# Seven block products instead of eight for a decoder layer's convolution operands and gates, with the gates kept in DRAM

## The chip, the cores and the metric

The kernel runs on one core of a Trainium2 chip. The metric is the device time of one execution in microseconds (us). Before the change it is 2046.91 us, the median of three runs (2045.77 to 2047.66).

## What is computed

One decoder layer for a prompt of 1024 tokens and 8 sample tokens, all in float32. The model width is 1024, and the 1032 tokens are the columns of every product below. Cut to what matters here:

```
p = h @ w_in                                # -> q | k | v | c_b | c_c | c_h | g_a | g_c
u = c_c * c_h
c = (c_b * causal_conv3(u)) @ w_conv_o
a = merge_of_three_attention_groups(q, k, v) @ w_attn_o
mix = (sigmoid(g_a) * a + sigmoid(g_c) * c) @ w_o
x = x + rms_norm(mix)
y = x + rms_norm(square(relu(rms_norm(x) @ w_ff1)) @ w_ff2)
```

Outputs are y for both groups, the updated key and value caches (for the samples a large copy from the input caches with one new row), and the last rows of u.

## The kernel before, in words

Every weight tile is 128 outputs of one matrix by 512 inputs (half of the 1024). `fetch` (L121) loads it with SP (256 KB, at most three raw tiles ahead). `split` (L129) makes two parts of it, so that three fast matmuls give float32 accuracy: ACT casts the high part (`wh`, L134), DVE or POOL subtracts to get the low part (`wl`, L135). The activations are held in two parts as well (`hh`, `hl` for the normalised input). `mac` (L162) issues wh by hh (L165), wh by hl (L168), wl by hh (L169), each 128 by 128 by 344 columns, since the 1032 columns are done in three chunks. `project` runs one tile of 128 outputs: 8 blocks of inputs, 3 chunks, 3 matmuls, so 72 matmuls of 344 columns. `plan` is the list of all weight tiles in the order of use; `tick`, called once per unit of PE work, splits the next tile when a buffer is free (five in `wpool`, two more in `wextra`).

The stages stand one after the other:

- Attention, with projections put between its heads as filling work. The last head has four raw gates as filling (`gate_raw`, L447): the pre-activation is stored in `gc_d` in DRAM.
- Convolution: 24 tiles of w_in, three for each of 8 output tiles (c_c, c_h, c_b). ACT copies c_c, DVE multiplies c_h by it into `E`, two scalar_tensor_tensor operations (L920, L921) do the width-3 convolution, DVE multiplies by c_b, and the result is split into `cvh`, `cvl`. `sample_steps` is a generator with the sample tokens' attention; `drive` pulls a step of it at every second unit of PE work. POOL multiplies cache tiles by queries (L788) and by weights (L844), DVE reduces them (L793) and adds them (L853).
- `wco`: the convolution's output matrix, 8 tiles. Its gates come from `gc_d` (four, loaded on POOL's queue, L953) or are computed in place (four).
- `wao`: the attention's output matrix, 8 tiles of 36 matmuls, with 8 gates between them. At its head the attention's numerators and denominators are loaded (SP), multiplied, and split into `ah`, `al` (L994 to L1000).
- `wo` and the feed-forward part, which the change leaves alone.

`copy_piece` (L278) issues pieces of the cache copy, DRAM to DRAM, 1 MB each, on ACT's queue: 16 in the attention, 16 in the convolution, 8 in `wco`, 8 in `wao`, 9 later. Each engine runs its own instructions in the order in which they stand; the DMA queues of SP, ACT and POOL are in order as well.

Of the kernel before, what the change touches and what calls it, by code (L numbers as in the profile page):

```python
# [19 lines left out]
KT = 8  # L20
# [3 lines left out]
CH = T // 3  # L24
EPS = 1e-6
# [10 lines left out]
def tile_decoder_layer(  # L36
# [10 lines left out]
    gc_d = dram.tile([NRAW, P, T], F32, name="gc_d")  # L47
# [35 lines left out]
    warr = {"win": win, "wao": wao, "wco": wco, "wo": wo, "wf1": wf1, "wf2": wf2}  # L83
    plan = []

    def plan_tiles(name, *ms):
        plan.extend((name, m, i) for m in ms for i in range(warr[name].shape[2] // 4))
# [7 lines left out]
    plan_tiles("win", *range(36, 60))  # L95
    for i in range(KT):
        if i >= NRAW:
            plan_tiles("win", 60 + i)
        plan_tiles("wco", i)
    plan_tiles("win", 68)  # L100
    for i in range(KT):
        if i + 1 < KT:
            plan_tiles("win", 69 + i)
        plan_tiles("wao", i)
    plan_tiles("wo", *range(KT))
    plan_tiles("wf1", 0, 1, 2, 3)
    for pr in range(NP - 2):
        if pr:
            plan_tiles("wf1", 2 * pr + 2, 2 * pr + 3)
        plan.extend(("wf2", 2 * pr + a, hf) for hf in range(2) for a in range(2))  # L110
    plan_tiles("wf1", 2 * NP - 2, 2 * NP - 1)
    plan.extend(("wf2", 2 * pr + a, hf) for hf in range(2) for pr in (NP - 2, NP - 1) for a in range(2))
    plan.reverse()

    spaces = [[wpool, 5, 5]]
    raws, ready = [], []
    clock, turn = [0], [0]
    lo_eng = [nc.gpsimd]
    lo_pin = [lambda ins: ins]

    def fetch():  # L121
        if plan and len(raws) < 3:
            key = plan.pop()
            name, m, i = key
            raw = wpool.tile([P, 4, P], F32, name="wr", tag="wr", bufs=3)
            pin(nc.sync.dma_start(raw, warr[name][m][:, 4 * i:4 * i + 4, :]))
            raws.append((key, raw, clock[0]))
# [10 lines left out]
    def split_next():  # L138
        key, raw, _ = raws.pop(0)
        space = max(spaces, key=lambda e: e[2])  # L140
        turn[0] += 1
        ready.append((key, split(raw, space, lo_eng[turn[0] % len(lo_eng)], lo_pin[0])))

    def tick():
        clock[0] += 1
        if raws and clock[0] - raws[0][2] >= 2 and max(e[2] for e in spaces) > 0:
            split_next()
        fetch()

    def take(key):  # L150
        if not ready:
            if not raws:
                fetch()
            split_next()
        k, w = ready.pop(0)
        assert k == key, (k, key)
        return w
# [103 lines left out]
    hpool = h_stack.enter_context(tc.tile_pool(name="hpool", bufs=1))  # L261
# [16 lines left out]
    def copy_piece(n=1):  # L278
        for _ in range(n):
            if pieces:  # L280
                tc.keep_in_program_order(nc.scalar.dma_start(*pieces.pop(0)))


    with ExitStack() as st:
# [161 lines left out]

        def gate_raw(i):  # L447

            t = aw.tile([P, T], F32, name="vT", tag="v01", bufs=1)

            def use(c, ps):
                nc.scalar.copy(t[:, chunk(c)], ps)
            yield from project(("win", 60 + i), h_in, use)
            nc.scalar.dma_start(gc_d[i], t)
# [211 lines left out]
        def fill(h):  # L666
# [10 lines left out]
            else:  # L677
                for i in range(NRAW):
                    yield from gate_raw(i)
# [30 lines left out]

    def sample_steps(sp):
# [10 lines left out]
        for g in range(3):  # L722
            qt, kt = tile512(NB), tile512(NB)
            for i in range(2):
                ps = bank(at, [P, 4, 2, 64], "ps_tq")
# [10 lines left out]
        for i in range(3):  # L736
            ps = bank(at, [P, 4, 2, 64], "ps_tq")
# [63 lines left out]
        ps = bank(at, [P, 512], "ps_sm")  # L801
# [5 lines left out]
        ps = bank(at, [P, 512], "ps_sm")  # L807
# [15 lines left out]
        ps = bank(at, [P, 512], "ps_sm")  # L823
# [5 lines left out]
        po = bank(at, [P, 512], "ps_so")  # L829
# [44 lines left out]
        ps = bank(at, [P, 512], "ps_sm")  # L874
# [5 lines left out]
    W0 = 36  # L880
    cv_stack = ExitStack()
    cpool = cv_stack.enter_context(tc.tile_pool(name="cpool", bufs=1))
    ch_ = cpool.tile([P, KT, T], F32R, name="cvh")
    cl_ = cpool.tile([P, KT, T], F32R, name="cvl")
    spaces.append([ctx.enter_context(tc.tile_pool(name="wextra", bufs=1, side="right")), 2, 2])
    lo_pin[0] = pin
    with ExitStack() as st:
# [7 lines left out]
        E = cw.tile([P, 2 + T], F32, name="E")  # L895
        nc.vector.memset(E[:, 0:2], 0.0)
        steps = sample_steps(cw)
        lo_eng[:] = [nc.vector, nc.gpsimd]

        short = [None]  # L900

        def drive(g):
            for j, _ in enumerate(g):
                if j % 2 == 1 or short[0]:
                    short[0] = next(steps, None)
        for i in range(KT):
            cs_sb = cw.tile([P, T], F32, name="cs_sb", bufs=1)

            def use_c(c, ps):
                nc.scalar.copy(cs_sb[:, chunk(c)], ps)  # L910
            drive(project(("win", W0 + 3 * i), h_in, use_c))
            def use_h(c, ps):
                nc.vector.tensor_tensor(E[:, 2 + c * CH:2 + (c + 1) * CH], ps, cs_sb[:, chunk(c)], op=OP.mult)
            drive(project(("win", W0 + 3 * i + 1), h_in, use_h))
            nc.scalar.copy(up[:, i, :], E[:, NQ:NQ + 2])
            nc.scalar.copy(us[:, i, :], E[:, NQ + 2:])
            y = cw.tile([P, T], F32, name="yc", bufs=1)
            w0, w1, w2 = (cwt[:, j, i:i + 1] for j in range(3))
            nc.scalar.activation(y[:, 0:NQ], E[:, 0:NQ], AF.Copy, scale=w0)
            nc.vector.scalar_tensor_tensor(y[:, 0:NQ], E[:, 1:1 + NQ], w1, y[:, 0:NQ], op0=OP.mult, op1=OP.add)  # L920
            nc.vector.scalar_tensor_tensor(y[:, 0:NQ], E[:, 2:2 + NQ], w2, y[:, 0:NQ], op0=OP.mult, op1=OP.add)  # L921
            nc.vector.tensor_scalar(y[:, NQ:], stt[:, i, 0, :], w0, None, op0=OP.mult)
            nc.vector.scalar_tensor_tensor(y[:, NQ:], stt[:, i, 1, :], w1, y[:, NQ:], op0=OP.mult, op1=OP.add)
            nc.vector.scalar_tensor_tensor(y[:, NQ:], us[:, i, :], w2, y[:, NQ:], op0=OP.mult, op1=OP.add)

            def use_b(c, ps):
                nc.vector.tensor_tensor(y[:, chunk(c)], ps, y[:, chunk(c)], op=OP.mult)
                nc.scalar.copy(ch_[:, i, chunk(c)], y[:, chunk(c)])
                nc.vector.tensor_tensor(cl_[:, i, chunk(c)], y[:, chunk(c)], ch_[:, i, chunk(c)].bitcast(F32),
                                        op=OP.subtract)  # L930
            drive(project(("win", W0 + 3 * i + 2), h_in, use_b))
# [5 lines left out]
    W1 = W0 + 24  # L937
    m2_d = dram.tile([KT, P, T], F32, name="m2_d")

    def gate(pool, src, store):  # L940
        def use(c, ps):
            s = pool.tile([P, CH], F32, name="sg", tag="sg", bufs=4)
            nc.scalar.activation(s, ps, AF.Sigmoid)  # L943
            store[c] = s
        return project(src, h_in, use)

    lo_eng[:] = [nc.vector]
    with tc.tile_pool(name="sgc", bufs=1, side="right") as sgp:
        for i in range(KT):
            sg = {}  # L950
            if i < NRAW:
# [398 lines left out]
```

## Time and profile before

| what | before |
|---|---|
| median of three runs | 2046.91 us |
| the profiled execution, its own time | 2046.12 us |
| its span in the profile | 2043.3 us |
| mean granted clock of the TensorE | 0.987 of full speed |
| PE busy | 1992.4 us, 12845 instructions |
| DVE, ACT, POOL busy | 1065.7, 687.3, 513.9 us |
| DMA | 195.50 MB, mean 96 GB/s |

A profiled time is made of the span and 2.8 us around it. Engines: PE is the matmul, PEld its weight load, DVE the vector engine, ACT the scalar engine, POOL the GpSimd engine, SP the engine that issues most loads. Matmuls are pipelined, so a matmul's own duration overlaps its neighbours', and what one costs is the distance between two starts. A granted clock of 1.00 is 2.4 GHz, one of 0.50 is 1.2 GHz.

### The profile page before, as it was taken

How to read it: one execution, taken by the hardware profiler on the slowest of the kernel's cores; microseconds unless marked ns; L12 is line 12 of the kernel's file. 1: busy time of each engine (PE TensorE's matmuls, PEld its weight loads, DVE VectorE, ACT ScalarE, POOL GpSimd, SP SyncE). 2: the span in 40 equal slices, each digit the busy share in tenths (PEclk: the TensorE clock that was granted, in tenths of full speed). 3: DMA queues.
4: the chain of work that ended last, by engine and by line, in shares of the span. 5: the costliest groups of instructions: out<-in, count | busy, mean ns of one | idle time of the engine just before them, and what ended most of it. 6: DMA issues, size and time to landing. Idle time of an engine off the chain costs nothing. (4 is left out here: it accounts for less than half of the span.)

```text
span 2043.3 us, 31854 instructions
## 1 busy us (share of the span) xinstructions
PE 1992.4 (98%) x12845; PEld 1971.1 (96%) x12845; DVE 1065.7 (52%) x1837; ACT 687.3 (34%) x1359; POOL 513.9 (25%) x414
## 2 busy tenths in 40 slices
PE   7999999999999999999989999899999999999997
PEld 6999999999999999999989999899999999999996
DVE  7688768777753454632223222825544444444445
ACT  4355435544443122222123233543222222222233
POOL 3233314332334433520013222312111111111113
PEclk8999999999999999999999999999999999999998
DMA  4221222123325644445364431322221111111112
GB/s 145 59 66 38 87 68 66 58 87 98 98 76 169 218 150 162 153 146 190 114 177 149 138 127 46 93 83 93 94 83 53 42 52 42 42 52 52 42 32 83
DMA packets 89667, 195.50 MB, mean 96 GB/s; under 512 B 23488, under 2 KB 33856, under 8 KB 88624
## 3 DMA queue, kind: packets, MB, share of 16 engines
q1 hardware_dynamic: 78144, 116.97, 18.2%
q10 hardware_dynamic: 6672, 63.49, 9.4%
q0 software_dynamic: 4704, 13.01, 2.1%
q8 instruction: 100, 1.64, 0.3%
q14 instruction: 47, 0.39, 0.1%
HBM read 173.60 MB, written 74.29 MB: 121 GB/s over the span
## 5 line engine op out<-in xcount | busy, mean ns | idle before, releaser
L165 PE MATMUL ps_mm<-hh,wh 128*128 128x344 f32 x1824 | 593.5, 325 | 4.7 <-ACT sg L943 2.2
L168 PE MATMUL ps_mm<-hl,wh 128*128 128x344 f32 x1824 | 586.5, 322 | 3.7 <-DVE hl L248 1.9
L169 PE MATMUL ps_mm<-hh,wl 128*128 128x344 f32 x1824 | 585.6, 321 | 0.0
L135 POOL TENSOR_TENSOR wl<-wr,wh 128x512 fp32r<-128x512 f32 x177 | 234.8, 1327 | 868.1 <-ACT wh L134 828.6
L134 ACT CAST wh<-wr 128x512 fp32r<-128x512 f32 x320 | 195.3, 619 | 568.9 <-PE ps_mm L168 477.0
L165 PEld LDWEIGHTS ps_mm<-hh,wh 128*128 128x128 f32 x1824 | 346.1, 190 | 7.4 <-ACT hh L254 2.9
L168 PEld LDWEIGHTS ps_mm<-hl,wh 128*128 128x128 f32 x1824 | 345.7, 190 | 6.0 <-DVE hl L248 3.2
L169 PEld LDWEIGHTS ps_mm<-hh,wl 128*128 128x128 f32 x1824 | 345.7, 190 | 0.0
L165 PE MATMUL ps_mm<-gh,wh 128*128 128x344 f32 x768 | 246.2, 321 | 0.0
L169 PE MATMUL ps_mm<-rh,wl 128*128 128x344 f32 x768 | 246.2, 321 | 0.0
L165 PE MATMUL ps_mm<-rh,wh 128*128 128x344 f32 x768 | 246.1, 320 | 0.0
L169 PE MATMUL ps_mm<-gh,wl 128*128 128x344 f32 x768 | 245.4, 319 | 0.0
L168 PE MATMUL ps_mm<-gl,wh 128*128 128x344 f32 x768 | 245.3, 319 | 0.0
L168 PE MATMUL ps_mm<-rl,wh 128*128 128x344 f32 x768 | 245.3, 319 | 0.0
L1187 DVE TENSOR_TENSOR f<-ps_mm,f 128x344 f32<-128x344 f32 x336 | 167.3, 513 | 97.0 <-PE ps_mm L169 96.8
L1125 DVE TENSOR_TENSOR r<-r 128x344 f32<-128x344 f32 x96 | 59.6, 621 | 215.9 <-ACT rh L1124 215.9
L135 DVE TENSOR_TENSOR wl<-wr,wh 128x512 fp32r<-128x512 f32 x143 | 99.9, 703 | 128.3 <-ACT wh L134 128.0
L168 PEld LDWEIGHTS ps_mm<-gl,wh 128*128 128x128 f32 x768 | 144.7, 188 | 0.0
L169 PEld LDWEIGHTS ps_mm<-gh,wl 128*128 128x128 f32 x768 | 144.7, 188 | 0.0
L165 PEld LDWEIGHTS ps_mm<-gh,wh 128*128 128x128 f32 x768 | 144.7, 188 | 0.0
L165 PEld LDWEIGHTS ps_mm<-rh,wh 128*128 128x128 f32 x768 | 144.5, 188 | 0.0
L169 PEld LDWEIGHTS ps_mm<-rh,wl 128*128 128x128 f32 x768 | 144.5, 188 | 0.0
(259 smaller groups left out, 2943.3 us busy)
## 6 DMA issues: line engine op xcount, KB each, us to landing
wr<-in_win_dram SPq DMA_DIRECT2D x152, 256.0 KB, 2.9
wr<-in_wf_dram SPq DMA_DIRECT2D x128, 256.0 KB, 2.8
out_okv_dram<-in_cache_dram ACTq DMA_DIRECT2D x16, 1020.0 KB, 8.1
kt<-in_cache_dram SPq DMA_DIRECT2D x32, 256.0 KB, 3.8
x_sb<-in_xT_dram SPq DMA_DIRECT2D x12, 344.0 KB, 5.4
m_d<-m POOLq DMA_DIRECT2D x8, 516.0 KB, 7.6
m2c<-m_d POOLq DMA_DIRECT2D x24, 172.0 KB, 3.6
xk<-in_xT_dram SPq DMA_DIRECT2D x12, 344.0 KB, 3.6
```

What stands on the lines that cost most here:

```text
L134: pin_(nc.scalar.copy(hi, raw))
L135: pin_(eng.tensor_tensor(lo, raw, hi.bitcast(F32), op=OP.subtract))
L165: ins = nc.tensor.matmul(ps, wh, rh, start=(first and i == 0), stop=False)
L168: nc.tensor.matmul(ps, wh, rl, start=False, stop=False)
L169: nc.tensor.matmul(ps, wl, rh, start=False, stop=(last and i == n - 1))
L1125: pin(nc.vector.tensor_tensor(r, r, r, op=OP.mult))
L1187: pin(nc.vector.tensor_tensor(d, ps, d, op=OP.add))
```

## The change

Two weight tiles (256 outputs) are taken together, with the inputs in two halves of 512 and the columns in two halves of 516 (`HT`), each done as two slices of 258 (`ST`). A product of two-by-two blocks then takes seven block products instead of eight (Strassen's scheme in the form with four sums of blocks on each side). This is done for 17 pairs: 12 of the convolution's operands (per two output tiles: two pairs "u", whose halves are multiplied together, and one pair "y" with the c_b of both), and 5 of gates ("g"). A pair is 7 products, each 2 slices by 4 blocks by 3 matmuls: 168 matmuls of 258 columns.

- The right-hand sums T1 to T4 are made once, from `hh` and `hl`, by `tsums` on DVE and POOL, while PE computes two gates in the old way (`plain`, tiles 68 and 69). T2, T3, T4 get buffers of their own, T1 takes the place of h in half of `hh` and `hl` (L995, L996), since the seven products read h itself only three times.
- The left-hand sums of a pair are four `combine` operations on POOL (L133): s1, s2, and two in place. Each of the seven forms is then split as before, the low part on DVE alone.
- `strassen` keeps three sums A, B, C in PSUM (two slices each, six banks); ACT copies A, DVE adds the others on the way out. All gates and the convolution's product go to DRAM (`g_d`, `cv_d`) in halves, on POOL's queue, and the attention's heads are split (`split_heads`) beside the last two gate pairs.
- Then `wao` runs first (its gates from `g_d` on POOL's queue, the convolution's product from `cv_d` on ACT's queue, split there), its result goes to `m2_d`, and `wco` follows, with gate and `m2_d` chunks loaded on POOL's queue.
- The cache copy's pieces: 16 in the attention, 30 in the pairs' stage, four together after the last pair, seven in `wao`.

```diff
+    def forms_of(key):
+        ...
+        def s2(r):
+            s[1] = combine("s1", r[0], r[2], OP.add)
+            s[2] = combine("s2", s[1], r[1], OP.subtract)
+            return s[2]
+        how = (((0, 1, 2), s2, ()), ((1,), lambda r: r[1], ()), ((), lambda r: s[1], ()),
+               ((0, 1), lambda r: combine(None, r[1], r[0], OP.subtract, r[0]), (0, 1)),
+               ((3,), lambda r: r[3], ()), ((2,), lambda r: r[2], (2,)),
+               ((3,), lambda r: combine(None, r[3], s[2], OP.subtract, s[2]), (3,)))
...
+        def tsums(j):
+            ...
+            V(b12, f32(hh[:, js, t2]), f32(hl[:, js, t2]), op=OP.add)
+            V(b22, f32(hh[:, ks, t2]), f32(hl[:, ks, t2]), op=OP.add)
+            V(T1[:, js], b12, f32(hh[:, js, t1]), op=S)
+            V(T1[:, js], T1[:, js], f32(hl[:, js, t1]), op=S)
+            V(T2, b22, T1[:, js], op=S)
+            parts(nc.vector, 2, T2)
+            yield
+            G(T3, b22, b12, op=S)
+            parts(nc.gpsimd, 3, T3)
+            yield
+            G(T4, f32(hh[:, ks, t1]), T2, op=S)
+            G(T4, T4, f32(hl[:, ks, t1]), op=OP.add)
+            parts(nc.gpsimd, 4, T4)
...
+    def strassen(pair, d, after=lambda p: None):
+        ...
+        for p in range(7):
+            w = take(("win", *pair, p))
+            acc = (B, A, C, B, A, B, C)[p]
+            for s in range(2):
+                ...
+                r = [x[:, :, ST * s:ST * s + ST] for x in RHS[p]]
+                for k in range(4):
+                    ins = nc.tensor.matmul(acc[s], w[0][:, k], r[0][:, k], start=(p < 3 and k == 0), stop=False,
+                                           skip_group_check=True)
+                    ...
+                    nc.tensor.matmul(acc[s], w[0][:, k], r[1][:, k], start=False, stop=False, skip_group_check=True)
+                    nc.tensor.matmul(acc[s], w[1][:, k], r[0][:, k], start=False, stop=(k == 3), skip_group_check=True)
+                if p == 1:
+                    pin(nc.scalar.copy(to(1, 0), A[s]))
+                    pin(nc.vector.tensor_tensor(to(0, 1), B[s], to(1, 0), op=OP.add))
...
+            run(heads)
+            copy_piece(4)
...
+                for i in range(KT):
+                    load_gate()
+                    load_cv()
+                    nc.scalar.activation(grs[i], grs[i], AF.Sigmoid)
+                    ...
+                    g = project(("wao", i), whole(ah, al), use_a)
+                    run(g, 1)
+                    for c in range(2):
+                        s = slice(HT * c, HT * c + HT)
+                        nc.scalar.copy(ch_[:, i, s], cvs[i][:, s])
+                        nc.vector.tensor_tensor(cl_[:, i, s], cvs[i][:, s], ch_[:, i, s].bitcast(F32), op=OP.subtract)
+                        run(g, 1)
+                    run(g)
+                    nc.gpsimd.dma_start(m2_d[i], grs[i])
+                    copy_piece(1)
```

How the order of instructions moves is shown at two places. The first is POOL between the attention and the first pair. Before, den_d (the denominators of the attention, sent to DRAM) is followed at once by its own way back and the next low part:

```order
L664 DMA den_d<-den_row 16x1x64
L714 DMA rdn<-den_d 128x64
L135 TENSOR_TENSOR wl<-wr,wh 128x512
L716 DMA rden_d<-rdn 128x64
L731 DMA sq_d<-kt 8x512
```

Now (T_6729 and T_6849 are T3 of the two halves, T_6730 and T_6850 are T4, s_6752 and s_6754 the first pair's s1 and s2; the first T3 and T4, three rows, stand ahead of den_d):

```order
L715 DMA den_d<-den_row 16x1x64
L133 TENSOR_TENSOR s_6752<-wr 128x512
L133 TENSOR_TENSOR s_6754<-s_6752,wr 128x512
L967 TENSOR_TENSOR t3l<-T_6729,t3h 128x1032
L977 TENSOR_TENSOR T_6849<-b_6847,b_6846 128x1032
L967 TENSOR_TENSOR t4l<-T_6730,t4h 128x1032
L980 TENSOR_TENSOR T_6850<-hh,T_6848 128x1032
L981 TENSOR_TENSOR T_6850<-T_6850,hl 128x1032
L967 TENSOR_TENSOR t3l<-T_6849,t3h 128x1032
L967 TENSOR_TENSOR t4l<-T_6850,t4h 128x1032
L133 TENSOR_TENSOR wr<-wr 128x512
```

The last row, the combine of the fourth form, stands behind all sums of T3 and T4 (its own way back of den_d comes after it). ACT's cast of that form stands in ACT's order ahead of the two casts that put T1 into `hh` (L995), and s1 and s2 wait until den_d has landed, because their buffers lie where the attention's were.

The second place is ACT's queue at the head of `wao`. Before, the pieces of the copy stand one by one between the tiles (here of `wco`; sg is a gate computed in place):

```order
L281 DMA out_okv_dram<-in_cache_dram 16x16384
L954 ACTIVATE gr<-gr 128x1032
L134 CAST wh<-wr 128x512 x2
L281 DMA out_okv_dram<-in_cache_dram 16x16320
L943 ACTIVATE sg<-ps_mm 128x344 x2
```

Now (out_okv is the cache copy, cv the convolution's product, gr a gate, cvh the high part of cv):

```order
L334 DMA out_okv_dram<-in_cache_dram 16x16384
L334 DMA out_okv_dram<-in_cache_dram 16x16320
L334 DMA out_okv_dram<-in_cache_dram 16x16384 x2
L1160 DMA cv<-cv_d 128x1032 x3
L1167 ACT_TABLE_LOAD
L1167 ACTIVATE gr<-gr 128x1032
L177 CAST wh<-wr 128x512
L1176 CAST cvh<-cv 128x516
```

Four pieces stand ahead of the first three loads of cv, and one more ahead of each of the five later loads; the cast of a cv stands in ACT's order ahead of later weight casts and of the next gate.

## Rows read from the trace of the kernel before

**Rows 1.** The page's parts 1 and 2, busy time of PE and granted clock in 40 slices.
```profile
PE 1992.4 (98%) x12845; PEld 1971.1 (96%) x12845; DVE 1065.7 (52%) x1837; ACT 687.3 (34%) x1359; POOL 513.9 (25%) x414
PEclk8999999999999999999999999999999999999998
```
**Rows 2.** Windows by stage: window, length, busy time (instructions) by engine, clock, DMA share, GB/s.
```profile
622.00:907.00 285.00, 281.53 (x1790) 276.56 (x1790) 138.93 (x205) 72.95 (x151) 113.56 (x91) 1.00 0.50 165
907.00:1043.00 136.00, 136.00 (x866) 136.00 (x867) 27.71 (x50) 25.30 (x43) 7.25 (x12) 1.00 0.49 159
1043.00:1193.00 150.00, 142.83 (x867) 140.89 (x866) 49.56 (x85) 43.11 (x83) 46.18 (x52) 0.95 0.55 159
...
1500.00:1600.00 100.00, 100.00 (x639) 100.00 (x638) 45.51 (x86) 23.14 (x45) 11.59 (x9) 1.00 0.22 69
```
**Rows 3.** Timeline of PE at the attention's last head: start, duration, instruction.
```profile
612.66 0.29 PE L607 MATMUL ps_c<-ph,V 128*128 128x256 f32 x1
612.78 0.28 PE L608 MATMUL ps_c<-pl,V 128*128 128x256 f32 x1
...
613.13 0.32 PE L165 MATMUL ps_mm<-hh,wh 128*128 128x344 f32 x1
```
**Rows 4.** Waits of PE from 1042 to 1090 us: total, times, longest.
```profile
PE ps_mm L165 <- ACT sg L943: 3.6, 2, 2.2
PE ps_mm L168 <- DVE al L1000: 2.3, 2, 1.9
PE ps_mm L165 <- ACT ah L999: 1.3, 1, 1.3
```
**Rows 5.** Windows around the half-clock stretch at the head of `wao`.
```profile
1062.00:1073.00 11.00, 8.85 (x31) 8.14 (x31) 5.87 (x10) 5.36 (x10) 3.96 (x3) 0.53 0.78 181
```
**Rows 6.** Timeline of DVE, then of POOL, from 649 to 655 us.
```profile
649.99 1.04 DVE L924 SCALAR_TENSOR_TENSOR yc<-us,cwt,yc 128x8 f32<-128x8 f32 x1 [0.36 <-ACT us L916]
651.05 2.28 DVE L920 SCALAR_TENSOR_TENSOR yc<-E,cwt,yc 128x1024 f32<-128x1024 f32 x1
653.37 1.28 DVE L921 SCALAR_TENSOR_TENSOR yc<-E,cwt,yc 128x1024 f32<-128x1024 f32 x1
...
649.71 1.30 POOL L135 TENSOR_TENSOR wl<-wr,wh 128x512 fp32r<-128x512 f32 x1 [3.86 <-ACT wh L134]
650.96 1.29 POOL L788 TENSOR_TENSOR kt<-kt,qb 128x512 f32<-128x512 f32 x1
```
**Rows 7.** Groups by form, 560 to 907 us: count, busy us, mean ns.
```profile
L596 POOL TENSOR_TENSOR den<-Sev,S1a 128x1024 f32<-128x1024 f32 x1 | 2.4, 2395 | 0.0
L532 DVE TENSOR_TENSOR tm<-tm,S2a 128x1024 f32<-128x1024 f32 x1 | 1.2, 1225 | 0.0
L534 DVE TENSOR_TENSOR tm<-tm,S1b 128x512 f32<-128x512 f32 x1 | 0.7, 692 | 0.0
...
L844 POOL TENSOR_TENSOR acc<-kt,ss 128x512 f32<-128x512 f32 x8 | 10.1, 1261 | 44.7 <-DVE accl L862 31.2 <-DMA kt<-in_cache_dram 13.5
L913 DVE TENSOR_TENSOR E<-ps_mm,cs_sb 128x344 f32<-128x344 f32 x24 | 12.4, 517 | 92.7 <-PE ps_mm L169 92.6
L793 DVE TENSOR_REDUCE ss<-kt 128x8 f32<-128x512 f32 x16 | 10.6, 674 | 0.0
```
**Rows 8.** From issue to landing: den_d (two transfers), a raw gate's store, the `wco` gates' loads.
```profile
DMA to landing us min/median/max: 2.1/4.5/6.9
...
DMA to landing us min/median/max: 3.4/3.4/3.4
...
DMA to landing us min/median/max: 5.8/8.5/9.6
```
**Rows 9.** Windows of 10 us with pieces of the copy: the last two columns are DMA share, GB/s.
```profile
622.00:632.00 10.00, 10.00 (x70) 9.50 (x70) 0.00 (x0) 1.24 (x3) 1.75 (x2) 1.00 0.85 316
662.00:672.00 10.00, 10.00 (x65) 10.00 (x65) 3.33 (x6) 1.68 (x4) 4.21 (x4) 1.00 0.88 304
912.00:922.00 10.00, 10.00 (x65) 10.00 (x64) 0.96 (x3) 3.34 (x5) 0.00 (x0) 1.00 0.72 250
```

More of the change, by code (lines that the diff above doesn't have):

```diff
@@ L138, in split_next, with loaded @@
     def split_next():
[L139 removed]
+        plan_key, keys, key, _, form, free = forms.pop()
+        rs = [raws.get((plan_key, k), (None,))[0] for k in keys]
         space = max(spaces, key=lambda e: e[2])
         turn[0] += 1
[L142 removed]
+        ready.append((key, split(form(rs), space, lo_eng[turn[0] % len(lo_eng)], lo_pin[0])))
+        for j in free:
+            raws.pop((plan_key, keys[j]))[2][2] += 1
+    def loaded(age):
+        plan_key, keys, _, of = forms[-1][0:4]
+        return all((plan_key, k) in raws and clock[0] - raws[plan_key, k][1] >= age for k in (keys[j] for j in of))
     def tick():
         clock[0] += 1
[L146 removed]
+        if forms and max(e[2] for e in spaces) > 0 and loaded(2):
             split_next()
@@ L150, in take @@
     def take(key):
-        if not ready:
-            if not raws:
+        while not ready:
+            if loaded(0):
+                split_next()
+            else:
+                n = len(loads)
                 fetch()
-            split_next()
+                assert len(loads) < n
         k, w = ready.pop(0)
@@ L935, in tile_decoder_layer @@
         nc.sync.dma_start(ust, us)
[L937 to L951, printed above, removed]
-                gr = sgp.tile([P, T], F32, name="gr", tag="gr", bufs=2)
-                nc.gpsimd.dma_start(gr, gc_d[i])
-                nc.scalar.activation(gr, gr, AF.Sigmoid)
-                sg = {c: gr[:, chunk(c)] for c in range(3)}
-            else:
-                run(gate(sgp, ("win", W1 + i), sg))
-            m2 = sgp.tile([P, T], F32, name="m2", bufs=2)
-            def use_cc(c, ps):
-                nc.vector.tensor_tensor(m2[:, chunk(c)], ps, sg[c], op=OP.mult)
-            run(project(("wco", i), whole(ch_, cl_), use_cc))
-            nc.gpsimd.dma_start(m2_d[i], m2)
-            copy_piece(1)
-    cv_stack.close()
     m_stack = ExitStack()
@@ new lines, in tile_decoder_layer @@
+            heads = split_heads()
+            for pair in gate_pairs:
+                D = [pre.tile([P, T], F32, name=f"D{a}") for a in range(2)]
+                if pair is gate_pairs[-1]:
+                    raw_spaces.pop()
+                for _ in strassen(pair, D, stores(D, [g_d[m - 60] for m in pair])):
+                    run(heads, 1)
+            run(heads)
+            copy_piece(4)
+        t_stack.close()
+        h_stack.close()
+        spaces.append([ctx.enter_context(tc.tile_pool(name="wextra", bufs=1, side="right")), 2, 2])
```

364 lines of the change are left out of this document (236 added, 128 removed).

## The prediction, made before the changed kernel had run

> **What bounds the kernel now.** I read the page first: PE is busy for 98% of the span, the other engines for about half of it or less [rows 1]. Then the windows by stage: in the convolution, `wco` and the feed-forward part PE hardly stops, so those stages cost what their matmuls cost, and only the stage from 1043 us loses time [rows 2]. In the feed-forward window 639 matmuls of 344 columns take 100.00 us, which is 156.5 ns each. In the timeline I looked for a narrower form and found four starts of 256 columns between 612.66 and 613.13 us, 117.5 ns each [rows 3]. So time here follows the columns closely, and fewer columns save time, as long as DVE, POOL and the queues keep up. That is what the rest of the reading is about: how POOL and DVE get on together [rows 6, 7], and how much the DMA can move [rows 9].
>
> **The matmuls.** Of conv and gates 34 tiles change form: 34 x 72 = 2448 matmuls of 344 columns, 2448 x 156.5 = 383.1 us, go. In come 17 x 168 = 2856 of 258 columns at 118.5 ns (117.5 and two columns more): 338.4 us. That is **-44.7 us**. Everything PE did besides stays.
>
> A rule of the Trainium skill speaks against this term: TensorE: Matmul & The Clock Gate, section Back-to-back issue gap, gives a sustained spacing of 81 ns at 128 columns and 131 ns at 512. By a straight line between these, an estimate, the old matmuls would cost 109 ns and the new 98, and the term would be about +13 us. The rows show 156.5 and 117.5 ns instead, so the sum goes by the rows.
>
> **The head of `wao`.** From 1043 to 1193 us PE has 864 matmuls to do, 135.2 us of 150.0: 14.8 us are lost. Part is waits for `ah`, `al` and for gates behind them on ACT [rows 4], part is a stretch at a granted clock of 0.53, near the 1.2 GHz level, after those waits [rows 5]. In the new kernel the heads are split beside the gate pairs, three steps after their loads, and nothing of this waits on PE's path: **-14.6 us** (at least half of it, if the splits are late beside a pair).
>
> **The sums T1 to T4.** PE reaches the end of the attention at about 622 us. The two plain gates cover 144 x 156.5 = 22.5 us, up to 644.6. Meanwhile DVE starts on the sums when the last raw gate's store has landed, 622.2 + 3.4 = 625.7 [rows 8]. What matters is how DVE and POOL run together. In [rows 6] an 8-column operation of DVE takes 1.04 us, and ends where POOL's 649.71 + 1.30 ends; the next takes 2.28 where the same form takes 1.28 alone, and it had POOL's next operation to wait for. So operations with two inputs from SBUF take turns with POOL's. A read from PSUM (517 ns throughout) or a reduction (674) shows nothing of it [rows 7].
>
> Until the third product can read T1 as its right-hand side, there stand in front: on POOL ten operations of 1032 columns (2.42 us, from 2395 ns at 1024) and three of 512 (1.28), 28.0 us; on DVE ten sums, two low parts of T2 and two of T1 (1.23 each) and five weight subtractions (0.69), 20.7 us. In turn that is 48.7 us, and 3.7 us of waiting for den_d to land in between (2.1 to 6.9 us) [rows 8], less about 1 us where a wait of one lies beside work of the other: 625.7 + 51.4 = 677 us. The first two products run earlier (5.7 us) and are hidden by this, so the third is late by 677 - 644.6 - 5.7 = 26.7 us. The next needs DVE to read out B first, which stands behind a load of conv weights in DVE's order, 2 to 3 us more: **+29 us**. If the two engines did not take turns, POOL's own chain would end at 664 and the casts of T1 at 669, and the term would be +22; if the late operations were reordered off the path it could be 12, and with a slow clock afterwards 36.
>
> **The pairs.** A pair is 168 x 118.5 = 19.9 us of PE. Operations that must take turns: DVE seven low parts (4.8 us); in a u pair two products of halves (1.4) and two convolution operations (2.6, and 0.2); in a y pair four products (2.8); POOL four combines, 5.1 us. So u is 14.1, y 12.7, g 9.9, all below 19.9. The sample tokens' steps come on top: their 24 weighted values fall on pairs 8 to 11 for the most part (u, u, y, g; 22 of them, from the order of POOL), POOL 22 x 1.2 = 26.4 us, DVE 22 sums and some 7 splits x 0.69 = 20 us. Together these four pairs have 50.8 + 46.4 = 97.2 us of turns, or 92 with the shortest products, against 79.6 us of PE. Of the 12 to 17 us, about 4.3 (one and a half products, for which PSUM has room) are absorbed: **+8 us** from the lower end, with ends 0 (the sample steps run late and fill the slack of the last pairs) and 25. What is late then is a low part `wl`, and PE waits for it. In the conv stage of before DVE and POOL together are busy for less than 90% of the window [rows 2], so it never met this.
>
> **From `wao` on.** All 8 loads of cv must have come before the first tile of `wco` ends. On ACT's queue 9 pieces stand ahead of the last (9.4 MB) and 8 cv (4.2); beside them run 8 gates (4.2), about 5 stores of m2 (2.6) and 12 weight tiles (3.1): 23.5 MB. With pieces in flight the DMA moved 316 GB/s at a share of 0.85, 304 at 0.88, 250 at 0.72 [rows 9], so 345 to 372 at full share: 63 to 68 us. A gate's load behind two pieces took up to 9.6 us [rows 8], and here there are four. Against that PE has `wao`, 288 x 156.5 = 45.1 us, and seven eighths of a chunk of `wco`, 3.3 us. So PE waits 15 to 20 us in all: **+18 us**, with ends 5 (pieces done earlier than their place suggests) and 33 (290 GB/s, as the third window's mix would fall to). It shows first as ACT waiting for cv, with the next weight cast queued behind it.
>
> For this the Trainium skill has two figures that differ: DMA: Bandwidth & Descriptors, Specifications, has about 358 GB/s from HBM for a core, and the table under Bandwidth 425 GB/s for a 16 MB load by one core alone. As estimates they would make 66 us and 55 us, PE's wait 17 or 7, and the total about 2041 or 2031. Rows show the first.
>
> At `wco` the loads of gates and m2 wait for the last m2 store while PE has four chunks ready: 0 (up to +3). The other edits (E in two buffers, the start of y, `hpool` on the other side) are on engines with room: 0.
>
> **The sum.** 2046.1 (the profiled execution, 0.8 below the median of 2046.9) - 44.7 - 14.6 + 29 + 8 + 18 = 2041.8, so **2042 us**. Below I call no change what lies within 0.2% (4 us) of 2046.9, about what a measurement can tell.
>
> **The rivals.**
> - *The covers hold*: the sums at 12 to 15, the pairs 0, `wao` 5 to 8: 2046.1 - 59.3 + 20 = about **2007 to 2015**. For it: no engine besides PE is over half busy on average [rows 1]. Against it: the order on POOL and ACT puts each wait on the path. Chance 0.18.
> - *No turns between DVE and POOL for these forms*: 22 + 1 + 18, **2028**. For it: most pairs of operations in the old stage do not collide. Against it: [rows 6]. Chance 0.14.
> - *The turns bound the pairs* (slower): if DVE and POOL lose a further tenth in changing over, the u pairs with query products (six of 1.28 on POOL, 21.8 us of turns) are over 19.9 as well, and the pairs lose 25 us instead of 8: 2042 + 17 = **2059**. It decides when more than 13 us are lost there. For it: in six of the twelve pairs in which sample steps run, the turns come to 100% of PE's time or more. Chance 0.17.
> - *The DMA is slower with four pieces in a row* (slower): at 290 GB/s the head of `wao` loses 33 us: **2057**. For it: the windows with pieces were never above 316 GB/s. Chance 0.10.
> - *258 columns cost as the line from 128 to 344 columns would have it* (some 135 ns): +47, **2089**. [Rows 3] at 256 columns speak against it. Chance 0.02.
> - The change does what it says as far as the counts go; the forecast itself has 0.39, of which about half lies within 4 us of the median or above it.
>
> **How the numbers follow.** Forecast 2042 with a range of its own of 2028 to 2056 from the ends 22 to 36, 0 to 25 and 5 to 33, which do not all fall on one side. Eight in ten: 2012 to 2062 leaves out the better half of the first rival, part of the third and the last. Faster by over 0.2% (below 2043): the first two rivals and half of the forecast, 0.52. Within 0.2%: 0.18. Slower: 0.30.
>
> **What would show it.** Right: 258-column starts 118 to 119 ns apart; one PE gap of over 20 us in the first product or the third, ended by DVE's `hl` of T1; PE in the late u and y pairs waiting for `wl` while DVE's long operations are stretched by POOL's; PE in `wao` waiting for DVE or ACT, these for cv, with the DMA share near 1. Wrong: PE continuous through the pairs, or cv landed well before 60 us after the last pair. A granted clock of about 0.5 after the first gap for more than 10 us would put the result above 2046.

## The result, and the profile after

The changed kernel takes 2118.22 us (median of four runs, 2112.52 to 2119.55); beside it the kernel before took 2047.29 us. The ratio is 1.0337, interval 1.0312 to 1.0362: **slower by 3.4%**, where I forecast 2042 us with a range up to 2062. The profiled execution took 2112.52 us, its span is 2110.3 us, 67.0 more than before, at a mean granted clock of 0.969 (0.987 before).

Parts 1 and 2 of the page of the changed kernel, to be read against [rows 1]:

```profile
PE 1971.2 (93%) x13253; PEld 1945.9 (92%) x13253; DVE 1236.2 (59%) x2081; ACT 733.1 (35%) x1448; POOL 601.2 (28%) x523
PEclk8999999999997889999988999999999999999998
```

PE has less to do, as the change wants, but 139 us of the span without work (51 before), and the clock dips in slices 13 to 15 and 21 to 22. The windows by stage, with the columns of [rows 2], say where: the sums T1 to T4 (645 to 680), the pairs (to 1100), the head of `wao` (1100 to 1168), `wco` behind it.

```profile
645.00:680.00 35.00, 17.08 (x88) 15.05 (x89) 18.61 (x28) 13.50 (x25) 28.20 (x22) 0.61 0.19 60
680.00:1077.00 397.00, 342.07 (x2664) 335.11 (x2663) 252.81 (x386) 106.94 (x218) 170.19 (x162) 0.93 0.55 187
1077.00:1100.00 23.00, 20.15 (x166) 19.75 (x165) 15.23 (x23) 9.65 (x16) 7.14 (x10) 1.00 0.60 178
1100.00:1168.00 68.00, 46.55 (x270) 45.43 (x269) 23.23 (x46) 20.95 (x32) 7.46 (x15) 0.85 0.94 347
1168.00:1264.00 96.00, 96.00 (x612) 95.84 (x611) 45.12 (x89) 30.46 (x64) 27.61 (x52) 1.00 0.52 159
1600.00:1700.00 100.00, 100.00 (x639) 100.00 (x639) 50.03 (x92) 21.68 (x42) 11.65 (x9) 1.00 0.15 48
```

`wco` and the feed-forward window run as they did. PE stands still, or at half clock, longer than before only where the change is. Three starts of the new form, from the timeline of PE:

```profile
685.69 0.28 PE L1015 MATMUL ps_a<-hl,wh 128*128 128x258 f32 x1
685.81 0.28 PE L1016 MATMUL ps_a<-hh,wl 128*128 128x258 f32 x1
685.93 0.28 PE L1011 MATMUL ps_a<-hh,wh 128*128 128x258 f32 x1
```

They stand 120 ns apart, so a pair of 168 takes 20.1 us. The 17 pairs, each from its first matmul to the first of the next, the last one to its own end, worked out from the starts in the trace (us, pair 0 first):

```
after  47.1  27.2 26.6 26.7 28.5 22.3 20.8 25.2 28.2 24.4 26.8 26.5 24.4  20.1 20.1  34.7 23.5
```

Pairs 13 and 14, where the sample steps are over and no head is split, cost exactly their matmuls. Pair 0 carries the sums T, pairs 15 and 16 the heads. What PE waited for from 640 to 1100 us, its longest five waits (total, times, longest):

```profile
PE ps_b L1011 <- DVE D L1019: 46.6, 12, 13.0
PE ps_b L1015 <- DVE t2l L967: 7.4, 1, 7.4
PE ps_tq L782 <- ACT kt L785: 7.0, 1, 7.0
PE ps_b L1011 <- DVE E L1021: 6.0, 3, 4.3
PE ps_b L1011 <- ACT wh L177: 4.5, 1, 4.5
```

One line leads: L1019, DVE's first read-out of the PSUM sum B, behind the second product. The fourth product goes on adding to B, so it may not start until B has been read. Each sum lies in two slices, so the room is one and a half products. Pair 13, which runs clean, has the last matmul of the second product's first slice, the read-out of both slices, and the first matmul of the fourth product:

```profile
1005.93 0.28 PE L1016 MATMUL ps_a<-hh,wl 128*128 128x258 f32 x1
...
1008.19 0.75 DVE L1019 TENSOR_TENSOR D<-ps_b,E 128x258 f32<-128x258 f32 x2
...
1010.35 0.29 PE L1011 MATMUL ps_b<-t3h,wh 128*128 128x258 f32 x1
```

From the end of the first (1006.21) to the start of the last are 4.1 us, and ACT's copy of A and DVE's addition must lie in them. That is all the room there is; the second read-out (L1021, ahead of the sixth product) and the third (L1026, ahead of the next pair's first) have as much. What DVE itself waited for before L1019, in the view of that line:

```profile
L1019 DVE TENSOR_TENSOR D<-ps_b,D x18: 407/417/428, 733.6 to 1089.1; 128x258 f32<-128x258 f32 x18
...
  DMA g_d<-D: 17.7, 3
  DMA cv_d<-D: 8.9, 3
...
  PE ps_b L1011: 46.6, 12
```

So DVE's wait there is mostly for a **store** (26.6 us, six times): the new pair writes its D where the old pair's last half still lies, on its way to DRAM. One case, timelines of POOL and DVE at pair 8:

```profile
876.90 0.58 POOL L1067 DMA_DIRECT2D g_d<-D  x1 [2.13 <-DVE D L1028]
...
884.07 0.76 DVE L1019 TENSOR_TENSOR D<-ps_b,E 128x258 f32<-128x258 f32 x2 [6.26 <-DMA g_d<-D]
```

The store is issued at 876.90 and DVE may write at 884.07, 7.2 us later; the quickest such store of that stretch landed in 2.4. The windows around it:

```profile
869.00:876.00 7.00, 5.50 (x46) 5.32 (x45) 4.11 (x7) 1.78 (x4) 4.23 (x4) 1.00 0.68 216
876.00:884.00 8.00, 4.26 (x36) 4.05 (x34) 1.80 (x4) 1.78 (x4) 0.58 (x1) 0.91 0.66 244
884.00:889.00 5.00, 4.46 (x20) 4.46 (x21) 2.56 (x5) 0.00 (x0) 2.27 (x2) 0.50 0.84 283
```

PE works 4.26 of 8 us, and after the gap it is granted 0.50, the 1.2 GHz level: the fourth product of this pair took 5.1 us. Beside the store ran two pieces of the cache copy. The DMA queues from 690 to 1100 us (q10 is the copy's queue, q0 POOL's), and the landing of the weights, which was 2.9 us before:

```profile
q10 hardware_dynamic: 960, 31.42, 21.1%
q0 software_dynamic: 3898, 13.09, 9.5%
...
wr<-in_win_dram SPq DMA_DIRECT2D x58, 256.0 KB, 5.5
```

31.42 MB in 960 packets are 32.7 KB in one, against 3.4 KB on POOL's queue. The Trainium skill (DMA: Bandwidth & Descriptors, Queues, rings and completion order) says that an SDMA engine goes round its queues and drains a whole packet of one before it turns to the next. The landings agree as far as they go; no run here changed the size of a packet.

### The profile page after: what moved, and what is told of

It reads as the page before. It is cut to its first block, busy times and chain, and to the rows that moved or that the text cites. A ratio compares the mean times of both kernels' runs of the same rounds, so it can differ in the third digit from the quotient of the medians.

```text
span 2110.3 us, 33274 instructions
## 1 busy us (share of the span) xinstructions
PE 1971.2 (93%) x13253; PEld 1945.9 (92%) x13253; DVE 1236.2 (59%) x2081; ACT 733.1 (35%) x1448; POOL 601.2 (28%) x523
## 4 chain that ended last, share of the span: by engine, by line
PE 48%; DVE 6%; DMA 6%; issue 4%; POOL 2%; ACT 1%; SPq 0%; ACTq 0%; DVEq 0%; POOLq 0%
PE ps_mm L218 14%; PE ps_mm L222 14%; PE ps_mm L221 14%; DVE wl L178 2%; DMA qb<-sq_d 1%; PE ps_b L1011 1%; PE ps_b L1015 1%; PE ps_b L1016 1%; DMA kt<-in_cache_dram 1%; DMA gr<-g_d 1%; POOL s L133 1%; DMA rden<-rden_d 1%; DMA g_d<-D 1%; DMA m_d<-gr 1%; PE ps_a L1011 1%
## 5 line engine op out<-in xcount | busy, mean ns | idle before, releaser
L178 POOL TENSOR_TENSOR wl<-wr,wh 128x512 fp32r<-128x512 f32 x152 | 201.8, 1328 | 803.6 <-ACT wh L177 703.2
L218 PE MATMUL ps_mm<-hh,wh 128*128 128x344 f32 x1008 | 329.6, 327 | 2.5 <-ACT hh L307 1.9
L221 PE MATMUL ps_mm<-hl,wh 128*128 128x344 f32 x1008 | 324.2, 322 | 3.7 <-DVE hl L301 1.9
L222 PE MATMUL ps_mm<-hh,wl 128*128 128x344 f32 x1008 | 323.3, 321 | 0.0
L178 DVE TENSOR_TENSOR wl<-wr,wh 128x512 fp32r<-128x512 f32 x168 | 149.9, 894 | 173.9 <-ACT wh L177 173.8
L221 PEld LDWEIGHTS ps_mm<-hl,wh 128*128 128x128 f32 x1008 | 190.7, 189 | 5.7 <-DVE hl L301 3.2
L218 PEld LDWEIGHTS ps_mm<-hh,wh 128*128 128x128 f32 x1008 | 191.1, 190 | 3.9 <-ACT hh L307 2.9
L222 PEld LDWEIGHTS ps_mm<-hh,wl 128*128 128x128 f32 x1008 | 190.8, 189 | 0.0
L221 PEld LDWEIGHTS ps_mm<-rl,wh 128*128 128x128 f32 x768 | 144.3, 188 | 0.0
```

The source lines that it names most:

```text
L178: pin_(eng.tensor_tensor(lo, raw, hi.bitcast(F32), op=OP.subtract))
L218: ins = nc.tensor.matmul(ps, wh, rh, start=(first and i == 0), stop=False)
L221: nc.tensor.matmul(ps, wh, rl, start=False, stop=False)
L222: nc.tensor.matmul(ps, wl, rh, start=False, stop=(last and i == n - 1))
```

## The experiments

Theories at this point: (A) the copy's pieces delay the stores and loads on which in-order queues wait; (B) DVE and POOL hold each other up, and POOL's order (sample products ahead of weight sums) makes the low parts late; (C) one buffer of D1 and D2 makes each pair wait for the store of the one before. All ratios are to the kernel before, run on the same chip, with 95% intervals.

**x1_copy_later.** No pieces in the pairs and in `wao`; 8 go to `wco`, the others to the feed-forward part (the words behind # say where a line stands).

```diff
-            copy_piece(2)          # each pair
-            copy_piece(4)          # after the last pair
-                    copy_piece(1)  # each wao tile
-            copy_piece(2)          # feed-forward
+            copy_piece(3)
```

> The changed kernel without pieces of the cache copy between the first pair and the end of wao (41 pieces moved: 8 stay in wco, the rest to the feed-forward part at three per step). Theory A, pieces hold up the other transfers (a D half's store, a query or cache tile, rden) and the in-order queues wait for these: the pairs after the first shrink from 406 us (694 to 1100) towards 16 x 20.1 = 322, to 330 to 350, and the 22 us lost in wao nearly go: 2118 becomes 2025 to 2045. Theory B, DVE and POOL taking turns: the pairs stay at 390 or more, only wao gains: 2090 to 2105. Theory C, the single buffers of D: the waits of DVE's read-out on D's store get shorter but stay, 1 to 2 us in 8 pairs: 2050 to 2070.

2074.68 us, 1.0139 (1.0117 to 1.0161): of 1.0337, the pieces' place makes 0.0198, **some 40 us**. By stretches: pairs 1 to 12 284.6 in place of 307.6 us, the two head pairs 49.2 for 58.2 (behind them PE now waits 2.7 us ahead of `wao`), `wao` 56.4 for 71.3. PE's wait for L1019 fell from 46.6 to

```profile
PE ps_b L1011 <- DVE D L1019: 20.7, 8, 6.0
```

The time lies in none of the three ranges: less went than A or C said, more than B. A holds, then, and is not all. It shows in the stores themselves: of the four stores of a y or g pair up to pair 14 it is the last, issued beside two pieces, that is late, 5.8 to 9.7 us in the changed kernel against at most 4.1 for the others. Here the last ones take 2.4 to 6.9 us; the longest, a cv_d store, runs beside loads of the samples' caches.

**b1_before_copy_later.** The same done to the kernel before (24 of its pieces to the feed-forward part).

> The kernel before with its pieces of the convolution and of wao moved in the same way (24 pieces to the feed-forward part). If pieces cost the old kernel something too, it is at the head of wao, where the heads' loads are late: 2047 becomes 2035 to 2044 by theory A; by theory B 2047 +- 2.

2042.51 us, 0.9983 (0.9973 to 0.9992). The place of 24 pieces cost the old kernel 0.17%, that of 41 costs the new one 2.0%. The waits above point to the new kernel's short room as the reason; how much the larger number of pieces adds, no run separates.

**x3_no_key_products** and **x4_no_combines** ask about POOL.

```diff
-            pin(nc.gpsimd.tensor_tensor(kt[0:n], kt[0:n], qb[0:n], op=OP.mult))      # x3
...
-        pin(nc.gpsimd.tensor_tensor(out, x, y, op=op))                               # x4, in combine
-        return out
+        return x
```

> The changed kernel with the 24 products of cached keys and queries on POOL left out (DVE reduces the key tiles as they come, so the sample tokens' scores are something else). They fall on pairs 1 to 5. Theory B, turns: those pairs get shorter by the 1.3 us of each product that DVE no longer waits for, 6 to 15 us in all, pairs 7 to 16 unchanged: about 2105. Theory A: POOL no longer stands waiting for query tiles (40 us of idle time), so the combines behind come in time; pairs 1 to 5 get shorter by 10 to 20 us, but the gap ahead of the fourth product after each two pieces stays in the pairs whose D waits for a store (3 and 4, as 7, 8, 11, 12): 2095 to 2108.

2097.72 us, 1.0252 (1.0224 to 1.028): within the range of A, below B's 2105.

> The changed kernel with the four sums of weight tiles of each pair left out (POOL adds nothing; raw tiles stand in their place, so the gates and the convolution are something else). Theory B, turns: 68 operations of 1.28 us are gone from the shared path, the pairs lose most of their excess: 2118 becomes 2060 to 2080. Theory A: only what waited for POOL's queue goes; gaps before the fourth product in pairs 3, 4, 7, 8, 11, 12, 15 stay at about 4 us or more: 2085 to 2110.

2080.18 us, 1.0166 (1.014 to 1.0192): at the upper end of B's range, below A's. The pairs of the two:

```
x3     46.2  20.1 22.8 24.6 20.2 20.2 20.8 27.4 27.3 26.0 25.5 26.6 26.7  20.1 20.1  35.3 23.9
x4     44.4  20.1 20.3 27.1 25.9 20.2 20.8 24.5 24.7 21.1 21.1 26.0 23.0  20.1 20.1  35.0 24.4
```

Without the key products pairs 1 to 5, beside which they stand, lose 7.4 us over their matmuls where they lost 30.8. That is more than turns were to give (6 to 15), and the trace of the changed kernel shows a second way. Waits of POOL from 640 and of DVE from 680 to 1100 us:

```profile
POOL kt L843 <- DMA qb<-sq_d: 40.2, 8, 14.3
...
DVE wl L178 <- ACT wh L177: 82.7, 30, 9.0
```

A key product waits in POOL's order for its query tile, and the weight sums stand behind it. At pair 1 the product starts at 706.92 after 14.3 us, the sums at 708.16 and 709.51, ACT's cast at 710.81, DVE's low part behind that, and behind the low part, at 712.51, the second read-out, for which PE waited 4.3 us. PE waits for no low part in pairs 1 to 16; it waits for the read-out that stands behind one.

Without the weight sums every pair after the first is within a microsecond of 20.1 except pairs 3 and 4, 7 and 8, 11 and 12, 15 and 16. But for the heads' loads and one of 6.1 us put down to ACT, DVE's long waits there are for stores (waits of DVE, 690 to 1050 us):

```profile
DVE D L1016 <- DMA cv_d<-D: 20.3, 3, 7.3
...
DVE D L1016 <- DMA g_d<-D: 12.6, 2, 6.3
```

They are the pairs that follow a y or g pair, which ends in stores. So B costs time, and what is left without it are waits for stores, as A and C have it. The two halves of B, turns and POOL's order, go together in x4, which doesn't separate them.

**x2_four_buffers.** D1, D2 and E from one ring of four.

```diff
-            D1 = cw.tile([P, T], F32, name="D1")
+            D1 = cw.tile([P, 2 + T], F32, name="D", bufs=4)[:, 0:T]
```

> The changed kernel with E, D1 and D2 taken in turn from four buffers of one size (no more memory), so that a pair writes no buffer that the pair before is still storing; pieces and all else as they are. Theory C, single buffers: the gap ahead of the fourth product goes in pairs 3, 4, 7, 8, 11, 12 (3.3 to 5.3 us each with the slow clock after some of them): 2118 becomes 2082 to 2095; pairs 15 and 16 keep their gap, since their buffers come from another pool. Theory A or B alone: DVE stands waiting there for something else as well (turns, combines), and less than 12 us is gained: above 2106.

2110.5 us, 1.0306 (1.0286 to 1.0327). By itself it gives some 6 us, which the interval of the changed kernel (from 1.0312) does not clear, and far less than C expected. The waits of PE show why; the last row is of the changed kernel:

```profile
PE ps_b L1011 <- DVE D L1019: 28.3, 6, 13.8
PE ps_b L1011 <- DVE D L1021: 25.7, 8, 6.5
...
PE ps_b L1011 <- DVE D L1021: 2.4, 2, 2.3
```

L1019 lost 18 us, and L1021, the read-out two products later, gained 17 (in the changed kernel it had 2.4 under D and, as shown above, 6.0 under E, which is now a D as well). The store was only the last of several late things.

**x5_sums_on_dve.** All of T1 to T4 on DVE, T4 behind T1's casts, the weight sums for later products held back until then.

```diff
-            G(T3, b22, b12, op=S)
-            parts(nc.gpsimd, 3, T3)
+            V(T3, tt[j][1], tt[j][0], op=S)
+            tparts(3, T3, js)
```

> The changed kernel with all of T1 to T4 made on DVE, T4 behind T1's casts, the forms from the fourth on held back until then, and den_d of the last head sent by SP. My account of the first pair (28 us of POOL and 20.7 of DVE take turns, and the cast of T1 stands behind POOL's last combine) makes of it 24 operations of 1.23 us on DVE, 30 us with the low parts from 624 us on: the first pair lasts 22 to 30 us instead of 47, 2118 becomes 2095 to 2102. If it were the wait for den_d or the loads of the conv weights that hold the first pair, at most 7 us go: above 2110.

2106.58 us, 1.0287 (1.0263 to 1.0311): the first pair went from 47.1 to 38.5 us, so about a third of the 27 us lost there goes with POOL taken out of the sums, den_d sent by SP and the weight sums held back, which this run doesn't separate. The time is neither in the range of my account (2095 to 2102) nor above 2110. The longest wait left is of PE's transposes of the samples, whose copy stands behind the casts of T on ACT (x10, below, takes it away):

```profile
PE ps_tq L784 <- ACT kt L787: 10.3, 1, 10.3
```

**x6_three_together.** x1, x2 and x5 at once.

> Pieces later (2075 alone), four buffers and the sums on DVE together. Where each removes its own wait: 2075 - 18 (gaps left in pairs 3, 4, 8, 11 of the first run) - 19 = 2038, 2030 to 2048, against 2046 of the kernel before. If the waits stand behind each other, so that one only uncovers the next: 2055 or more.

2056.37 us, 1.0047 (1.003 to 1.0064). The single gains (0.0198, 0.0031 and 0.0050) add up to 1.0058; so they neither help nor hinder each other much, and something is left that none of them touches. My 2038 had counted 18 and 19 us for two edits that had given some 6 and 10 alone.

**x7_steps_rarer.** x6 with a sample step at each third unit in place of two in five.

```diff
-                if beat[0] % 5 in (1, 3) or short[0]:
+                if beat[0] % 3 == 1 or short[0]:
```

> The three together, and the sample steps at every third unit of work instead of two in five. Turns and POOL's queue (theory B) still cost in pairs 5, 8, 9, 10, 11, where POOL's products, combines and DVE come to 100% or more of PE's time; at five sixths of the rate 4 to 8 us less than the run with the three: 2030 to 2034. If the turns cost nothing there: the same within 2 us.

2043.34 us, 0.9981 (0.9969 to 0.9994): 13 us from spreading the sample work, more than the 4 to 8 expected, and still above 2030 to 2034, since x6 had not come to 2038. Pairs 1 to 12 take 264.4 us, 23 above 12 x 20.1. In pairs 1 to 14 DVE waits for no store any more, so the store part of C is gone. What PE still waits for there, 12.6 us at the three read-outs, finds DVE at its own work, stretched beside POOL's, or waiting for a weight cast. Both timelines at pair 3:

```profile
726.64 0.58 POOL L1083 DMA_DIRECT2D cv_d<-D  x1 [2.85 <-DVE D L1082]
727.25 1.30 POOL L845 TENSOR_TENSOR kt<-kt,qb 67x512 f32<-67x512 f32 x1
728.49 1.28 POOL L134 TENSOR_TENSOR s<-wr,s 128x512 f32<-128x512 f32 x1
729.73 1.29 POOL L845 TENSOR_TENSOR kt<-kt,qb 128x512 f32<-128x512 f32 x1
730.97 1.26 POOL L134 TENSOR_TENSOR s<-wr 128x512 f32<-128x512 f32 x1
...
727.46 5.33 DVE L179 TENSOR_TENSOR wl<-wr,wh 128x512 fp32r<-128x512 f32 x1
732.71 0.74 DVE L1035 TENSOR_TENSOR D<-ps_b,D 128x258 f32<-128x258 f32 x2
```

A subtraction that takes 0.69 us takes 5.33: it begins after the first of four POOL operations that follow each other without a gap, and ends 0.6 us after they have ended (732.23). Behind it stands the read-out that PE needs; the window says 6.00 of 6 us for DVE, 5.94 for POOL and 3.68 for PE:

```profile
727.00:733.00 6.00, 3.68 (x31) 3.48 (x29) 6.00 (x3) 1.00 (x2) 5.94 (x7) 0.99 0.48 167
```

**x10_samples_after_pair0, x9_heads_ahead, x8_all_with_wao** build on x7, one step each.

```diff
+                if beat[0] > 14 and (beat[0] % 11 in (1, 4, 7, 9) or short[0]):           # x10
+                    ar = pre.tile([P, NQ], F32, name="num", bufs=2)                       # x9
+                        grs.append(sga.tile([P, T], F32, name="gr", bufs=6))              # x8
```

> As x7, with the sample work beginning only after the first pair (then 4 times in 11 units) and the clearing of E's first two columns on DVE in place of POOL. In x7 PE's transposes of the samples (ps_tq) wait 8.9 us in the first pair for an ACT copy that stands behind the casts of the T sums. Theory 'each gap has its own queue': that wait goes, the first pair falls from 36.5 to 26 to 29 us and the time by 8 to 10 us against x7, to 2032 to 2036. Theory 'waits stand behind each other': the T sums themselves are then late for PE, the first pair stays above 33, or the denser sample work later takes it back, and the time stays above 2039.

2049.54 us, 1.0014 (1.0001 to 1.0028): 6 us worse than x7. The wait for ACT's copy went, and the first pair still takes 35.8 us: now DVE's read-out stands behind T4's sums, 10.0 us long. And pairs 1 to 14 took 8 us more (316.4 for 308.8), with denser sample steps and with E cleared on DVE, for which (L1090) PE waits 3.8 us. Here the theory of waits behind each other was right. PE's waits for that read-out from 640 to 1035 us:

```profile
PE ps_b L1027 <- DVE D L1035: 15.6, 4, 10.0
```

> x10 with the head division's loads a round ahead (two num tiles; the next rden loaded right behind the product). Theory 'own queue': pair 15 falls from about 27 to 20 to 22 us and the time by 5 to 7 us against x10. Rival 'the transfers are slow in that stage, not the queues': pair 15 stays above 25 and the time within 2 us of x10.

2041.91 us, 0.9975 (0.9963 to 0.9986). The median fell by 7.6 us; in the profiled execution pairs 15 and 16 went from 48.7 to 44.5, and a wait of 2.7 us ahead of `wao` went with it. Pair 15 is at 24.4, between what the two theories said, so the loads' order was part of its wait, and a part is left.

> x9 with six gate and six convolution buffers in wao in place of four, three units loaded ahead in place of two. In x7 wao took 55.4 us for 48 x 8 x 3 x ... PE work of about 45, with ACT's sigmoid waiting 18.7 us on the gate loads and the weight casts behind it. Theory 'own queue': wao falls to 47 to 50 and the time by 5 to 8 us against x9. Rival 'the first load bounds it': the first gate arrives no sooner, wao stays above 53 and the time within 2 us of x9.

2039.34 us, 0.9955 (0.9938 to 0.9971): 2.6 us, and `wao` at 51.9 us in place of 55.5: between what the two theories gave; the interval overlaps that of x9.

**x11_taps_later.** x7 with the head loads and the buffers of x9 and x8; the convolution's taps issued later.

> x7 (not x10) with the head loads ahead and the six buffers in wao, and the convolution's three DVE products of a u pair issued behind the next pair's first read-out of B in place of ahead of it. From x10 to x9 the heads gave 7.6 us and from x9 to x8 wao gave 2.6, so these two alone would bring x7's 2043 to about 2033. Theory 'DVE's queue order makes the gaps behind u pairs' (pairs 5, 10 and 13 of x7, 24.3, 25.7 and 22.9 us): these pairs fall to 20 to 22 and the time to 2022 to 2028. Rival 'DVE and POOL taking turns makes them, whatever stands in the queue': the gap comes back at the next product, the sum of pairs 1 to 14 stays within 4 us of x7's (310 us) and the time at 2030 to 2036.

**2030.84 us, 0.9924** (0.9903 to 0.9944): the fastest kernel here, 0.76% faster than the one before, also faster than b1. What I expected of heads and `wao` alone was 2033, which the interval holds, and pairs 1 to 14 take 309.4 us, as the rival said. The taps are not settled all the same (times of the profiled execution, the slowest of the six): pair 10 fell from 25.7 to 23.1, pairs 5 and 13 rose from 24.3 to 26.2 and from 22.9 to 24.1, and in pair 5 the trace has both taps (780.50 and 783.38) still ahead of the read-out (785.58), as in pairs 2, 6, 9 and 14, so the edit didn't reach DVE's order there. Its windows, T, pairs, and `wao`:

```profile
648.00:686.00 38.00, 27.56 (x210) 25.67 (x209) 27.36 (x46) 17.58 (x40) 16.68 (x25) 0.87 0.18 56
686.00:1039.00 353.00, 335.04 (x2714) 330.36 (x2714) 271.06 (x397) 112.32 (x220) 179.45 (x160) 0.99 0.41 132
1039.00:1090.00 51.00, 47.18 (x283) 46.89 (x283) 28.45 (x52) 23.15 (x35) 9.04 (x17) 0.93 0.83 299
```

## Why the prediction was wrong

The sign was wrong: of the forecast's terms four came out near what was said, one of them by luck, and two failed. From the attention's last matmul to the first of `wo` the kernel before takes 570.9 us (621.8 to 1192.7) and the new one 642.6 (619.6 to 1262.2), 71.7 more; the rest of the kernel gives back 4.7.

- **The matmuls** (-44.7): right but for 1.5 ns. 120 in place of 118.5 ns makes it -40.4.
- **The old head of `wao`** (-14.6): it went, as said.
- **The sums T** (+29): the size was right, the way only in part, so the size is luck. The first pair took 47.1 us, 27.0 above its matmuls, and its third product began at 676.7 us, where my working has 677. But T1's low part, for which I had it wait, was ready at 670.9. PE had lost the time before that: ahead of the first product to a weight cast (4.5 us, to 647.1), in the first product to T2's low part (7.4 us in the waits above, beside POOL's sums), in the second to the samples' transposes (7.0), with the half clock behind them (0.61 from 645 to 680). DVE's timeline has one low part of T2 stretched to 3.38 us (1.23 alone), and the last two low parts of T1, together 2.38 us, done at 670.87:

```profile
654.75 3.38 DVE L967 TENSOR_TENSOR t2l<-T,t2h 128x1032 fp32r<-128x1032 f32 x1
...
668.49 2.38 DVE L996 TENSOR_TENSOR hl<-T,hh 128x1032 fp32r<-128x1032 f32 x2 [0.18 <-ACT hh L995]
```

- **The pairs** (+8, at most 25): **this step failed**. Pairs 1 to 12 took 307.6 us, 66.4 over 12 x 20.1. About 5 us of that is PE's own work for the samples, 24 matmuls that the old kernel has between its tiles too, so some 61 us stand against my 8. Of the 66.4 PE was idle for 41.6, and some 20 are matmuls that ran slower behind the gaps: 41 us of this stretch have a granted clock of 0.50, the 1.2 GHz level. Three things were wrong in it. First, one and a half products of room was right in size (4.1 us), but I took it once from a sum over four pairs; it is the room at each read-out of B, and a delay beyond it is lost each time, however idle DVE is afterwards. Second, I saw to it only that work in turns fits, and not what DVE's read-out waits for in DVE's order: the old pair's store, and the pieces that slow it (x1: 23 us in these pairs), and a low part whose weight sum stands on POOL behind a waiting key product (x3: 23 us in pairs 1 to 5). I put the loss on pairs 8 to 11 and none on pairs 1 to 5, though my own 21.8 us of turns in a u pair with key products are over 19.9. The copy's 30 pieces in the pairs I had priced for `wao` alone. Third, a turn isn't one POOL operation long (x7: 4.6 us behind four). My rival of the turns had the right engines but a time of 2059.
- **The heads** (0): **failed**, +18, of which 6 to 9 go with the pieces (x1). I wrote that nothing of this waits on PE's path. The division stands in DVE's queue, and DVE waits in it for a load; behind it stands PE's read-out. Waits of DVE from 680 to 1100 us, and its timeline:

```profile
DVE num L1119 <- DMA rden<-rden_d: 15.6, 1, 15.6
...
1061.58 1.23 DVE L1119 TENSOR_TENSOR num<-num,rden 128x1024 f32<-128x1024 f32 x1 [15.56 <-DMA rden<-rden_d]
1063.32 0.75 DVE L1019 TENSOR_TENSOR D<-ps_b,D 128x258 f32<-128x258 f32 x2
```

  PE's longest wait for L1019, 13.0 us, is this one. I should have asked, of a step moved beside PE's work, whom its queue holds up.
- **From `wao` on** (+18, up to 33): `wao` took 71.3 us to `wco`'s first matmul against 45.1 of matmuls, +26. The amount moved was right: 347 GB/s over 68 us are 23.6 MB, I had 23.5 at 345 to 372 GB/s (the 290 of my upper end has no row behind it). 15 of the 26 go with the pieces (x1). Through whom it shows was not right: not cv, but the gates, the later of which are loaded only when an m2 store has given their buffer back (landed at 1149.33, load issued at 1149.85). Waits of ACT, then of PE, 1100 to 1172 us:

```profile
ACT gr L1167 <- DMA gr<-g_d: 34.2, 5, 12.6
...
PE ps_mm L218 <- DVE gr L1171: 21.5, 4, 12.7
```

The sum by its own terms: -40.4 - 14.6 + 5.0 (the two plain gates and the wait behind them, 27.5 us from 619.6 to 647.1 in place of 22.5) + 27.0 + 66.4 + 18.0 + 26.2 = +87.6. Two things in it the old stage had as well: the 60 matmuls of the samples, 8.6 us, and 6 us lost in its convolution (285.0 us, against 279.0 for 1728 matmuls and these 60). That leaves +73.0; +71.7 was measured in that stage. The slow clock is inside each term. One slip of the working changes nothing here: the first rival's upper end is 2010 by its own terms, not 2015.

What stays open: how much of the 23 us left in x7's pairs is DVE held by POOL and how much is late weight sums and landings behind them, since no run took POOL out of a kernel without pieces; and whether the taps matter.

## What to carry to other kernels

When a change shortens the work that covers everything else, look for the place with the least room between a result and its next use, here one and a half products, 4.1 us, and list all that its reader's in-order queue can wait for there: other engines' buffers, stores, loads of unrelated steps. Sums of work over a stage say nothing of it. The bulk copies cost 0.17% in the kernel with slack and 2.0% in the one without, so they are moved first; then the background steps are thinned. With four buffers, the sums on DVE and earlier loads of the heads besides, this made a 3.4% loss a 0.8% gain with the same matmuls.

## What was not expected of the hardware

- DVE can be passed over by POOL more than once. With POOL's operations back to back, a 0.69 us subtraction of DVE took 5.33 us, through four of them; in the changed kernel 16 of the 112 weight subtractions on DVE between 690 and 1100 us took over 1.3 us, up to 3.87. In the same stretches reads from PSUM stayed at 0.41 to 0.43 us. The Trainium skill (SBUF — State Buffer, SBUF: two separate sides) has the two engines' shared ports as a lock that one instruction holds whole while the other blocks. The stretched rows agree; that the waiting one is passed over by several is what the rows of x7 add.
- A store of 258 KB that landed in 2.3 us at best took up to 9.7 beside copies from DRAM to DRAM and weight loads. Around pair 8 one landed in 2.4 us and the next in 7.0, at DMA shares of 0.68 and 0.66: it is not the mean share alone that tells what a transfer waits for.
- The gap of 4.3 us at pair 8 was followed by a stretch at the 1.2 GHz level (0.50 from 884 to 889 us), so this wait cost PE half as much again: the product behind it took 5.1 us in place of 2.9.
